# The opening of a decoder-trunk kernel: weight tiles in halves, squares summed by TensorE, two streamed columns, a new fixed order

## The chip, the cores and the metric

The kernel runs on one core of a Trainium2 chip. The time is the device time of one execution in microseconds (us). A core has four compute engines that run their own instruction lists side by side and wait for each other by semaphores: TensorE (PE: matrix products; its weight loads are listed as PEld), VectorE (DVE), ScalarE (ACT) and GpSimd (POOL). SyncE (SP) and POOL here mainly issue DMA transfers. PE writes its results into PSUM banks, which DVE and ACT read; everything else lies in SBUF, on 128 partitions.

## The reference

A trunk of two layers over 512 tokens of width 1024, all in float32. Each layer has three sub-layers, each added to the residual: a SwiGLU feed-forward, a mixing of the tokens, and a second SwiGLU feed-forward. Ahead of each stands an RMS norm whose scale and shift come from a vector `c`:

```python
c_act = jax.nn.silu(c)
for l in range(DEPTH):
    mod = (c_act @ w_ada[l] + b_ada[l]).reshape(B, N_MOD, D_MODEL)
    sh1, sc1, gt1, sh2, sc2, gt2, sh3, sc3, gt3 = [mod[:, i, None, :] for i in range(N_MOD)]
    hn = rms_norm(h, g_ffn1[l]) * (1.0 + sc1) + sh1
    h = h + 0.5 * (1.0 + gt1) * swiglu(hn, w_ffn1_in[l], w_ffn1_out[l])
    hn = rms_norm(h, g_mix[l]) * (1.0 + sc2) + sh2
    ...   # attention over a window, RWKV-7, a short convolution, side by side; w_mix_out
    hn = rms_norm(h, g_ffn2[l]) * (1.0 + sc3) + sh3
    h = h + 0.5 * (1.0 + gt3) * swiglu(hn, w_ffn2_in[l], w_ffn2_out[l])
```

The change touches only the way to the first `hn` of the first layer and the first six of the 44 output tiles of `hn @ w_ffn1_in[0]`.

## The kernel before

All activations lie transposed: `h` and `hn` are eight blocks (k = 0 to 7) of 128 columns of the model by 512 tokens. A product is made to float32's precision out of three products in a shorter format: the weight and the activation are each split into a high part (a cast on ACT) and the rest (a subtraction on DVE), and PE adds wH·xH, wH·xL and wL·xH. In the steady part `split` (lines 139 and 141) makes the parts of a weight tile of 128x1024 and `mm3` (lines 127 to 129) the three products. One output tile is thus 8 blocks times 3, or 24, matmuls of 128x128 by 512.

The opening, `begin` (line 1317 on), comes ahead of all this and is written out by hand. Its steps are tokens of a table, `PLAN`; `step` turns a token into instructions, and `pin` chains each to the one ahead of it on its engine, so that the table is the order. What the tokens do:

- `R0` spreads the 512 values 1/rms to all partitions (PE, line 1415). Ahead of it, in plain code, ACT and DVE square the blocks of `h`, DVE adds the eight squares up (line 1375), PE sums over partitions (line 1380), ACT takes the root (1382) and DVE the reciprocal of 128x4 values (1383).
- Scale and shift of the columns of block k come by one of two ways. For a *streamed* column: `ada`k multiplies c by a megabyte of `w_ada` on PE (1437), `part`k copies the sums (ACT, 1440), `col`k adds them over partitions (PE, 1444), and `gm`k finishes the scale and the shift (`finish`, DVE, lines 1389 and 1390). For a *dotted* one: `d`k and `e`k are two dot products on DVE (1394), of 128x1024 each, with `crep`, silu(c) spread to all partitions; `e`k ends with `finish` too.
- `z`k multiplies block k of `h` by 1/rms (DVE, 1420), `x`k applies scale and shift (ACT, 1422), `H`k and `L`k split the result (ACT 1424, DVE 1426).
- `wH`n and `wL`n split weight tile n (ACT 1430, DVE 1432). `P`nk and a letter is one matmul of output tile n (line 1409): a is wH·xH, b is wH·xL, c is wL·xH. There are 6 x 8 x 3 = 144 of them; the last wL·xH of the last tile ends the opening on PE, and the next tile's matmuls, of lines 127 to 129, follow.
- `W` and a number are so many products of ones, which nobody reads (line 1350). `s`k is silu over a half of `crep`. `more` names the loads that are issued behind a token.

The loads of the opening stand on SP's queue alone: `h` in four of 512 KB, eight of 1 MB of `w_ada` (`wada`) and six weight tiles of 512 KB (`wfirst`, five buffers). Behind the opening, ACT and DVE work through the splits of the next weight tiles (`wraw`), silu and products of the finished tiles (lines 520 to 524), and dot products with `w_ada` for the later norms (line 197), in an order which the program's scheduler sets from the code's order and its priorities.

Of the kernel before, what the change touches and what calls it, by code (L numbers as in the profile page):

```python
# [33 lines left out]
ada0 R0 part0 s0 col0 z0 wH0 ada1 gm0 z5 x0 z4 part1 z1 H0 W2 col1 z7 s1 P00a wH1 gm1 z3 x1 L0 W4 P10a ada2 z6 wH2 z2 H1 P00b wL2 P10b P20a part2 P20b  # L34
P01a wH3 col2 L1 P20c P11a gm2 P30a P30b wL3 x2 P01b P11b P21a P21c H2 P21b d3 P31a P30c P31b P31c P02a P12a L2 P22a P22c P32a e3 P02b P12b P22b wH4
P32c P32b wL0 W1 P40a x3 P40b P41a P41b P42a H3 P42b d4 P00c P01c P02c P03a P03c L3 P13a wH5 P23a P23c P33a e4 P03b P13b P50a P50b P51a P51b P52a wL5
x4 P52b P23b P33c P33b H4 P43a d5 P43b P50c P51c P52c P53a P53b L4 P53c P04a P04c e5 P14a P04b P14b P24a P24c P24b P34a P34c wL4 x5 P34b P44a P44b
P54a H5 P54c d6 P54b P40c P41c P42c P43c P44c L5 P05a P05c P15a e6 P05b P15b P25a P25c P25b P35a P35c wL1 P35b x6 P45a P45c P45b P55a H6 P55c d7 P10c
P11c P12c P13c P14c P15c L6 P55b P06a P06c e7 P06b P16a P16c P16b P26a P26c P26b x7 P36a P36c P36b P46a H7 P46c P46b P56a P56c L7 P56b P07a P07c P07b
P17a P17c P17b P27a P27c P27b P37a P37c P37b P47a P47c P47b P57a P57c P57b  # L40
""".split()
GROUPS = ((0, 12), (12, 22))
# [26 lines left out]
def trunk_kernel(ctx, tc, ins, out, layers=L, phases=("ffn1", "mix", "ffn2")):  # L69
# [1247 lines left out]
    def begin(pool):  # L1317
# [13 lines left out]
        wa, wf = [], []  # L1331

        def fetch():
            w = pool.tile([P, 2 * D], F32, name="wada", tag="wada", bufs=4)
            nc.sync.dma_start(w, ins["wa0"][len(wa)])
            wa.append(w)

        def fetch_w():
            j, g = divmod(len(wf), 2)
            w = pool.tile([P, KD, P], F32, name="wfirst", tag="wfirst", bufs=5)  # L1340
            nc.sync.dma_start(w, ins["w1i"][0, j, g])
            wf.append(w)
# [16 lines left out]
        for k in range(KD):  # L1359
            pin("PE", mm(turned[k // 4][:, k % 4], cT[:, k : k + 1].to_broadcast([P, P]), cst("ident"), start=True, stop=True))  # L1360
        warm(22)
        ss, sqs = new_ss(), {}
        sqs[0] = ss
        for i in range(KD):
            if i in (3, 4):
                x = pool.tile([P, T], F32, name="sqs", tag=f"sq{i}")
            else:
                x = E("sq") if i else ss
            sqs[i] = x
            if i == 3:  # L1370
                pin("DVE", tt(x, h[i], h[i], ALU.mult))
            else:
                pin("ACT", act(x, h[i], AF.Square))
        for a, b in ((0, 1), (0, 2), (0, 3), (4, 5), (4, 6), (4, 7), (0, 4)):
            pin("DVE", tt(sqs[a], sqs[a], sqs[b], ALU.add))
        for f in (fetch, fetch_w, fetch, fetch_w, fetch_w, fetch, fetch_w, fetch):
            f()
        pt = psum([P, NB], "ps_ss")
        for b in range(NB):
            pin("PE", mm(pt[:, b : b + 1], ss[:, b * P : (b + 1) * P], ones[:, :1], start=True, stop=True))  # L1380
        r = pool.tile([P, NB], F32, name="rstd_t", tag="rstd_t")
        pin("ACT", act(r, pt, AF.Sqrt, bias=vals["eps"], scale=1.0 / D))
        pin("DVE", nc.vector.reciprocal(r, r))
        rstd = psum([P, T], "ps_rstd", "r1")
        pin("DVE", stt(col["gb"], bsc, 1.0, g1, ALU.add, ALU.mult))
# [10 lines left out]
        more = {"ada0": (fetch, fetch_w), "ada1": (fetch,), "wL0": (fetch_w, fetch), "e3": (fetch,)}  # L1396

        def step(token):
            kind = "P" if token[0] == "P" else token.rstrip("0123456789")
# [3 lines left out]
            if kind == "P":  # L1403
                n, k, p = int(k[0]), int(k[1]), "abc".index(k[2])
                if n not in pts:
                    pts[n] = psum([P, T], "ps_mm", ("r0", "r1", "mm")[n % 3])
                w, x = ws[n][p == 2][:, k], weave(hn[k][p == 1])
                first, last = (token == ends[n][e] for e in range(2))
                latest["large"] = pin("PE", mm(paired(pts[n]), w, x, start=first, stop=last, skip_group_check=True))  # L1409
                return  # L1410
            k = int(k)
            c = slice(k, k + 1)
            if kind == "R":
                for b in range(NB):
                    pin("PE", mm(rstd[:, b * P : (b + 1) * P], r[:, b : b + 1].to_broadcast([P, P]), cst("ident"), start=True, stop=True))
            elif kind == "s":
                pin("ACT", act(crep[:, k * 512 : k * 512 + 512], turned[k].rearrange("p k n -> p (k n)"), AF.Silu))
# [7 lines left out]
            elif kind == "L":  # L1425
                pin("DVE", nc.vector.tensor_sub(hn[k][1], zs[k], hn[k][0].bitcast(F32)))
            elif kind == "wH":
                home, bufs = (wp, 4) if k < 4 else (pool, 2)
                ws[k] = tuple(home.tile([P, KD, P], F32R, name=x, tag=x, bufs=bufs) for x in ("wH", "wL"))
                pin("ACT", nc.scalar.copy(ws[k][0], wf[k]))  # L1430
            elif kind == "wL":
                pin("DVE", nc.vector.tensor_sub(ws[k][1], wf[k], ws[k][0].bitcast(F32)))
            elif kind == "ada":
                sums[k] = psum([P, 2 * P], "ps_ada")
                for i in range(KD):
                    j = slice(i % 4 * 32, i % 4 * 32 + 32)
                    pin("PE", mm(sums[k][j], cz[:, i], wa[k][:, i * 2 * P : (i + 1) * 2 * P], start=i < 4, stop=i >= 4))
            elif kind == "part":
                part[k] = pool.tile([P, 2 * P], F32, name="part", tag="part", bufs=2)
                pin("ACT", nc.scalar.copy(part[k], sums[k]))  # L1440
            elif kind == "col":
                sums[k] = psum([P, 2], "ps_col")
                for i in range(2):
                    pin("PE", mm(sums[k][:, i : i + 1], part[k][:, i * P : (i + 1) * P], ones[:, :1], start=True, stop=True))
            elif kind == "gm":
                finish(c, sums[k][:, :1], sums[k][:, 1:])
            elif kind == "d":
                dot(k, "sc", 0)
            elif kind == "e":
                dot(k, "sh", D)  # L1450
                finish(c, col["sc"][:, c], col["sh"][:, c])
            for f in more.get(token, ()):
                f()
# [42 lines left out]
def lay_out(i):  # L1496
# [12 lines left out]
    a["wa0"] = c(np.concatenate([streams[:3], wT[0, 1::-1, 3:].transpose(1, 2, 0, 3).reshape(5, P, 2 * D)]))  # L1509
# [67 lines left out]
```

## Time and profile before

| | |
|---|---|
| three timed runs | 1805.3, 1805.43 and 1809.03 us, median 1805.43 us |
| the profiled execution | 1807.22 us, of which the span of the profile is 1805.5 us |
| clock granted to PE, mean | 0.997 |
| PE / DVE / ACT / POOL busy | 98% / 75% / 47% / 8% of the span |
| first matmul of the opening's six tiles | starts at 19.37 us |
| last of them | starts at 59.84 us; the next section's first starts at 60.06 us |

The rows in the prediction are of a profiled execution. In a timeline a row gives the start and the duration in us, the engine, the line of the kernel, the operation, output<-input, the size, and the number of instructions that are drawn together; square brackets give the idle time before it and what ended it. PE's rows overlap: a matmul of 512 columns is shown with 0.38 us, while the next one starts 0.215 us after it. In the rows by windows the numbers are the length, the busy time of PE, its weight loads, DVE, ACT and POOL (with counts), the granted clock, the share of the DMA engines that is busy, and GB/s.

### The profile page before, as it was taken

To read this page: it belongs to the slowest core of one execution; us is meant where nothing else is said; L and a number is where in the kernel's file an instruction comes from. 1 tells how busy PE (TensorE), PEld (TensorE's weight loads), DVE (VectorE), ACT (ScalarE), POOL (GpSimd) and SP (SyncE) were. 2 spreads that over 40 slices of the span, in tenths; PEclk is the share of its full clock that TensorE was granted. 3 is DMA by queue.
4 is the path that set the end of the run, shared out by engine and by line. 5 is a ranking of instruction groups with operands and counts; after the bars stand their busy time and mean duration, and the time that the engine had idled before them with its cause. 6 is when DMAs were issued, how large, how long until landed. Compare 5 with 4: busy or idle time off the path is not lost.

```text
span 1805.5 us, 33687 instructions
## 1 busy us (share of the span) xinstructions
PE 1774.8 (98%) x13848; PEld 1616.9 (90%) x13848; DVE 1350.3 (75%) x2187; ACT 840.9 (47%) x1295; POOL 142.5 (8%) x227
## 2 busy tenths in 40 slices
PE   8999999999999999999999999999999999999999
PEld 6889899987778999899899989999876798999998
DVE  6688587877767977677888776887686788864862
ACT  5353255374443554255355524544654345533541
POOL 0101010101000001100100020110000000010000
PEclk9999999999999999999999999999999999999999
DMA  8667876623123576967737687773421427684742
GB/s 342 218 176 232 243 201 197 228 65 103 54 88 120 150 200 193 291 181 206 246 108 200 180 290 204 195 231 105 122 73 32 141 79 198 186 245 132 198 141 71
DMA packets 91405, 309.93 MB, mean 172 GB/s; under 512 B 10417, under 2 KB 11185, under 8 KB 90225
## 3 DMA queue, kind: packets, MB, share of 16 engines
q1 hardware_dynamic: 61920, 201.58, 32.9%
q0 software_dynamic: 29328, 106.18, 23.5%
q8 instruction: 109, 1.79, 0.4%
q14 instruction: 48, 0.39, 0.1%
HBM read 303.79 MB, written 3.93 MB: 170 GB/s over the span
## 4 chain that ended last, share of the span: by engine, by line
PE 81%; DVE 9%; DMA 4%; ACT 4%; issue 3%; POOL 0%; SPq 0%; ACTq 0%; DVEq 0%; POOLq 0%
PE ps_mm L127 13%; PE ps_mm L128 13%; PE ps_mm L129 13%; PE ps_d L431 7%; PE ps_d L433 7%; PE ps_d L432 7%; PE ps_f L433 3%; PE ps_f L431 3%; PE ps_f L432 3%; PE ps_g L433 2%; PE ps_g L431 2%; PE ps_g L432 2%; DVE wL L141 2%; PE ps_mm L1409 1%; ACT wH L139 1%
## 5 line engine op out<-in xcount | busy, mean ns | idle before, releaser
L139 ACT CAST wH<-wraw 128x1024 fp32r<-128x1024 f32 (+2 forms) x290 | 263.9, 916 | 465.8 <-PE ps_mm L128 212.4
L141 DVE TENSOR_TENSOR wL<-wraw,wH 128x1024 fp32r<-128x1024 f32 (+2 forms) x290 | 305.5, 1058 | 123.3 <-ACT wH L139 122.0
L127 PE MATMUL ps_mm<-actH,wH 128*128 128x512 f32 (+1 forms) x784 | 281.0, 358 | 0.0
L129 PE MATMUL ps_mm<-actH,wL 128*128 128x512 f32 (+1 forms) x784 | 280.6, 358 | 0.3 <-DVE wL L141 0.3
L128 PE MATMUL ps_mm<-actL,wH 128*128 128x512 f32 (+1 forms) x784 | 280.5, 358 | 0.0
L127 PE MATMUL ps_mm<-hnH,wH 128*128 128x512 f32 (+1 forms) x712 | 246.8, 353 | 1.7 <-ACT hnH L289 1.3
L128 PE MATMUL ps_mm<-hnL,wH 128*128 128x512 f32 (+1 forms) x712 | 246.2, 348 | 0.1
L129 PE MATMUL ps_mm<-hnH,wL 128*128 128x512 f32 (+1 forms) x712 | 244.8, 346 | 0.6 <-DVE wL L141 0.6
L431 PE MATMUL ps_d<-comH,wH 128*128 128x256 f32 x816 | 225.2, 276 | 0.8 <-ACT s L457 0.7
L432 PE MATMUL ps_d<-comL,wH 128*128 128x256 f32 x816 | 224.4, 275 | 0.0
L433 PE MATMUL ps_d<-comH,wL 128*128 128x256 f32 x816 | 224.4, 275 | 0.0
L141 DVE TENSOR_TENSOR wL<-sum,wH 128x1024 fp32r<-128x1024 f32 x102 | 124.9, 1225 | 81.0 <-ACT wH L139 80.8
L197 DVE SCALAR_TENSOR_TENSOR wada<-wada,crep 128x1024 f32<-128x1024 f32 x128 | 153.2, 1219 | 29.2 <-DMA wada<-in_wadaT 28.9
L129 PEld LDWEIGHTS ps_mm<-actH,wL 128*128 128x128 f32 x784 | 148.7, 190 | 17.5 <-DVE wL L141 0.7
L127 PEld LDWEIGHTS ps_mm<-actH,wH 128*128 128x128 f32 x784 | 148.7, 190 | 16.8 <-ACT wH L139 0.2
L128 PEld LDWEIGHTS ps_mm<-actL,wH 128*128 128x128 f32 x784 | 148.7, 190 | 16.6
L431 PEld LDWEIGHTS ps_d<-comH,wH 128*128 128x128 f32 x816 | 156.6, 192 | 2.3 <-ACT s L457 2.3
L433 PEld LDWEIGHTS ps_d<-comH,wL 128*128 128x128 f32 x816 | 156.7, 192 | 0.0
L432 PEld LDWEIGHTS ps_d<-comL,wH 128*128 128x128 f32 x816 | 156.6, 192 | 0.0
L139 ACT CAST wH<-sum 128x1024 fp32r<-128x1024 f32 x102 | 106.8, 1047 | 104.6 <-PE ps_f L432 42.4
L127 PEld LDWEIGHTS ps_mm<-hnH,wH 128*128 128x128 f32 x712 | 133.1, 190 | 22.0 <-issue 7.9
L129 PEld LDWEIGHTS ps_mm<-hnH,wL 128*128 128x128 f32 x712 | 135.4, 190 | 14.0 <-DVE wL L141 1.0
(389 smaller groups left out, 3861.0 us busy)
## 6 DMA issues: line engine op xcount, KB each, us to landing
wada<-in_wadaT POOLq DMA_DIRECT2D x128, 512.0 KB, 4.8
wraw<-in_wmi SPq DMA_DIRECT2D x40, 512.0 KB, 3.6
wraw<-in_w2p SPq DMA_DIRECT2D x36, 512.0 KB, 3.8
wraw<-in_w1p SPq DMA_DIRECT2D x32, 512.0 KB, 4.3
wraw<-in_w1o SPq DMA_DIRECT2D x32, 384.0 KB, 4.4
wraw<-in_w2o SPq DMA_DIRECT2D x32, 384.0 KB, 4.6
wraw<-in_w1o SPq DMA_DIRECT2D x32, 320.0 KB, 3.7
wraw<-in_w2o SPq DMA_DIRECT2D x32, 320.0 KB, 3.4
```

Source lines behind the costliest of these rows:

```text
L127: mm(acc, wH, xH, start=start, stop=False)
L128: mm(acc, wH, xL, start=False, stop=False)
L129: latest["large"] = mm(acc, wL, xH, start=False, stop=stop)
L139: nc.scalar.copy(hi, src)
L141: return nc.vector.tensor_sub(lo, src, hi.bitcast(F32))
L197: stt(w, w, 1.0, crep, ALU.mult, ALU.mult, accum_out=out_)
L431: mm(acc, wH, xH, start=start and i + k == 0, stop=False, skip_group_check=True)
L432: mm(acc, wH, xL, start=False, stop=False, skip_group_check=True)
L433: mm(acc, wL, xH, start=False, stop=k == 3, skip_group_check=True)
L1409: latest["large"] = pin("PE", mm(paired(pts[n]), w, x, start=first, stop=last, skip_group_check=True))
```

## The change

Eight things change, all in `begin` and in `lay_out`, the host's layout of the inputs; line numbers of the later functions move by two.

1. Weight tiles are loaded and split in halves of four blocks (128x512; token `wH3a` is the first half of tile 3): 12 loads of 256 KB instead of 6 of 512 KB, in six buffers. All loads of the opening are pinned on SP in a new order.
2. PE sums the squares: for each block four products with ones of 128x32, into four groups of 32 rows of one bank (`ps_ss`). The seven additions on DVE go. DVE squares three blocks instead of one. 1/rms is now a tile of 128x128, so the root and the reciprocal run over 128 columns instead of 4.
3. Two columns are streamed instead of three; block 2 is now dotted, which makes 12 dot products instead of 10.
4. ACT finishes scale and shift (two instructions of 128x1) instead of DVE.
5. silu is applied to c before it is spread, so `crep` is copied out plainly; the load of ACT's table for silu, formerly in the opening, comes at the first silu behind it.
6. 22 warm products ahead of the sums become 1, 2 and 5; later ones become `W2` and `W3`.
7. The six tiles' PSUM banks are (r0, r0, mm, r1, r1, mm) instead of r0, r1, mm in turn; tile 4 takes over the bank of `ps_rstd`.
8. `PLAN` is new.

```diff
-ada0 R0 part0 s0 col0 z0 wH0 ada1 gm0 z5 x0 z4 part1 z1 H0 W2 col1 z7 s1 P00a wH1 gm1 z3 x1 L0 W4 P10a ada2 z6 wH2 z2 H1 P00b wL2 P10b P20a part2 P20b
...
+R0 ada0 z2 wH1a z0 wH3a z6 part0 z7 W2 col0 wL1a gm0 x0 z1 W3 ada1 wL3a H0 z3 wH5a P10a P10c P30a z5 part1 P30c wH0a P50a wL5a col1 wH2a P00a L0 P50c
...
+HALF = {"a": slice(0, KD // 2), "b": slice(KD // 2, KD)}
+BANK = ("r0", "r0", "mm", "r1", "r1", "mm")
...
-            pin("PE", mm(turned[k // 4][:, k % 4], cT[:, k : k + 1].to_broadcast([P, P]), cst("ident"), start=True, stop=True))
-        warm(22)
...
-        for a, b in ((0, 1), (0, 2), (0, 3), (4, 5), (4, 6), (4, 7), (0, 4)):
-            pin("DVE", tt(sqs[a], sqs[a], sqs[b], ALU.add))
-        for f in (fetch, fetch_w, fetch, fetch_w, fetch_w, fetch, fetch_w, fetch):
-            f()
-        pt = psum([P, NB], "ps_ss")
-        for b in range(NB):
-            pin("PE", mm(pt[:, b : b + 1], ss[:, b * P : (b + 1) * P], ones[:, :1], start=True, stop=True))
...
+            pin("PE", mm(turned[k // 4][:, k % 4], cact[:, k : k + 1].to_broadcast([P, P]), cst("ident"), start=True, stop=True))
+        pss = psum([P, P], "ps_ss")
+        sqs = {}
         for i in range(KD):
...
+            sqs[i] = pool.tile([P, T], F32, name="sqs", tag="z", bufs=KD)
+            if i in (3, 5, 7):
+                pin("DVE", tt(sqs[i], h[i], h[i], ALU.mult))
...
+                pin("ACT", act(sqs[i], h[i], AF.Square))
+            for b in range(NB):
+                pin("PE", mm(pss[32 * b : 32 * b + 32], ones[:, :32], sqs[i][:, b * P : (b + 1) * P], start=i == 0, stop=i == KD - 1))
+            if i in (2, 4):
+                k = i // 2 - 1
+                pin("ACT", nc.scalar.copy(crep[:, k * 512 : k * 512 + 512], turned[k].rearrange("p k n -> p (k n)")))
+            if i in (3, 5):
+                warm((i - 1) // 2)
+        for token in "a0 w1a w3a a1 w5a w0a w2a a2 w4a a3".split():
+            fetch(token)
+        warm(5)
+        r = pool.tile([P, P], F32, name="rstd_t", tag="rstd_t")
...
-            pin("DVE", stt(col["gm0"][:, c], sc, g1[:, c], col["gb"][:, c], ALU.mult, ALU.add))
-            pin("DVE", tt(col["sh0"][:, c], sh, bsh[:, c], ALU.add))
+            pin("ACT", act(col["gm0"][:, c], sc, AF.Identity, bias=col["gb"][:, c], scale=g1[:, c]))
+            pin("ACT", act(col["sh0"][:, c], sh, AF.Identity, bias=bsh[:, c]))
...
-        more = {"ada0": (fetch, fetch_w), "ada1": (fetch,), "wL0": (fetch_w, fetch), "e3": (fetch,)}
+        more = {"ada0": "a4 w5b", "ada1": "a5 w4b w1b w2b", "e2": "a6 w3b w0b", "e3": "a7"}
...
-                    pin("PE", mm(rstd[:, b * P : (b + 1) * P], r[:, b : b + 1].to_broadcast([P, P]), cst("ident"), start=True, stop=True))
...
+                    pin("PE", mm(rstd[:, b * P : (b + 1) * P], cst("ident")[:, 32 * b : 32 * b + 1].to_broadcast([P, P]), r, start=True, stop=True))
...
-    a["wa0"] = c(np.concatenate([streams[:3], wT[0, 1::-1, 3:].transpose(1, 2, 0, 3).reshape(5, P, 2 * D)]))
+    a["wa0"] = c(np.concatenate([streams[:2], wT[0, 1::-1, 2:].transpose(1, 2, 0, 3).reshape(6, P, 2 * D)]))
```

The next rows are PE's list from its first instruction to the first matmul of the six tiles, before the change. `ps_crep` is the spreading of c, `ps_ss` the sum of squares, `ps_ada` and `ps_col` the two steps of a streamed column, `ps_rstd` the spreading of 1/rms.

```order
L1350 MATMUL ps_warm<-ones_r 128x512 x3
L1360 MATMUL ps_crep<-con,cT 128x128 x8
L1350 MATMUL ps_warm<-ones_r 128x512 x22
L1380 MATMUL ps_ss<-ones_r,ss 128x1 x4
L1437 MATMUL ps_ada<-wada,cz 32x256 x8
L1415 MATMUL ps_rstd<-con,rstd_t 128x128 x4
L1444 MATMUL ps_col<-ones_r,part 128x1 x2
L1437 MATMUL ps_ada<-wada,cz 32x256 x8
L1350 MATMUL ps_warm<-ones_r 128x512 x2
L1444 MATMUL ps_col<-ones_r,part 128x1 x2
L1409 MATMUL ps_mm<-hnH,wH 128x512
```

The same stretch of PE's list after the change:

```order
L1361 MATMUL ps_crep<-con,cact 128x128 x8
L1371 MATMUL ps_ss<-sqs,ones_r 32x128 x16
L1351 MATMUL ps_warm<-ones_r 128x512
L1371 MATMUL ps_ss<-sqs,ones_r 32x128 x8
L1351 MATMUL ps_warm<-ones_r 128x512 x2
L1371 MATMUL ps_ss<-sqs,ones_r 32x128 x8
L1351 MATMUL ps_warm<-ones_r 128x512 x5
L1425 MATMUL ps_rstd<-rstd_t,con 128x128 x4
L1439 MATMUL ps_ada<-wada,cz 32x256 x8
L1351 MATMUL ps_warm<-ones_r 128x512 x2
L1446 MATMUL ps_col<-ones_r,part 128x1 x2
L1351 MATMUL ps_warm<-ones_r 128x512 x3
```

The sums of squares now stand right behind the spreading of c, between a few warm products; the spreading of 1/rms stands ahead of the first streamed column instead of behind it, and the second column's `ps_ada` (the next row, not shown) comes behind the first column's `ps_col`.

On DVE, the rows right behind the opening before the change are these. `wL` is the rest of a weight tile's split, `silu` and `actL` belong to the finished output tiles, and `mod` is a result of the dot products with `w_ada` for a later norm:

```order
L141 TENSOR_TENSOR wL<-wraw,wH 128x1024
L522 SCALAR_TENSOR_TENSOR silu<-silu,ps_mm 128x512 x3
L524 TENSOR_TENSOR actL<-silu,actH 128x512 x3
L141 TENSOR_TENSOR wL<-wraw,wH 128x1024 x2
L197 SCALAR_TENSOR_TENSOR wada,mod_2_571<-wada,crep 128x1024 x3
L221 TENSOR_TENSOR mod_2_571<-mod_2_571,par 128x2
L141 TENSOR_TENSOR wL<-wraw,wH 128x1024
```

And after it:

```order
L143 TENSOR_TENSOR wL<-wraw,wH 128x1024
L524 SCALAR_TENSOR_TENSOR silu<-silu,ps_mm 128x512 x3
L526 TENSOR_TENSOR actL<-silu,actH 128x512
L143 TENSOR_TENSOR wL<-wraw,wH 128x1024
L526 TENSOR_TENSOR actL<-silu,actH 128x512
L199 SCALAR_TENSOR_TENSOR wada,mod_2_582<-wada,crep 128x1024
L526 TENSOR_TENSOR actL<-silu,actH 128x512
L199 SCALAR_TENSOR_TENSOR wada,mod_2_582<-wada,crep 128x1024 x2
L223 TENSOR_TENSOR mod_2_582<-mod_2_582,par 128x2
L143 TENSOR_TENSOR wL<-wraw,wH 128x1024
```

The split of the third weight tile behind the opening, which stood right behind the second's, now stands behind the three dot products.

More of the change, by code (lines that the diff above doesn't have):

```diff
@@ L1409, in step @@
                 latest["large"] = pin("PE", mm(paired(pts[n]), w, x, start=first, stop=last, skip_group_check=True))
+                return
+            if kind in ("wH", "wL"):
+                n, part_ = int(k[0]), HALF[k[1]]
+                if n not in ws:
+                    home, bufs = (wp, 4) if n < 4 else (pool, 2)
+                    ws[n] = tuple(home.tile([P, KD, P], F32R, name=x, tag=x, bufs=bufs) for x in ("wH", "wL"))
+                wH, wL, w = (x[:, part_] for x in (*ws[n], wf[n]))
+                if kind == "wH":
+                    pin("ACT", nc.scalar.copy(wH, w))
+                else:
+                    pin("DVE", nc.vector.tensor_sub(wL, w, wH.bitcast(F32)))
                 return
@@ L1445, in step @@
             elif kind == "gm":
-                finish(c, sums[k][:, :1], sums[k][:, 1:])
+                finish(c, *((sums[k][:, :1], sums[k][:, 1:]) if k in sums else (col["sc"][:, c], col["sh"][:, c])))
             elif kind == "d":
@@ L1450, in step @@
                 dot(k, "sh", D)
-                finish(c, col["sc"][:, c], col["sh"][:, c])
-            for f in more.get(token, ()):
-                f()
+            for load in more.get(token, "").split():
+                fetch(load)
         ends = {n: [[t for t in PLAN if t[:2] == f"P{n}"][e] for e in (0, -1)] for n in range(6)}
```

59 lines of the change are left out of this document (20 added, 39 removed).

## The prediction

> **What bounds the kernel now.** PE is busy for 98% of the span, so I first asked where it stands still or does what need not be done. The chain of waits, cut to the opening, gives the one long piece that is not PE's:
>
> ```profile
> 24.29 11.93 DMA wfirst<-in_w1i
> 36.24 1.05 ACT wH L1430
> 37.33 21.61 PE ps_mm L1409 x91
> ```
>
> The sixth weight tile is awaited for 12 us; behind its cast PE runs to the end of the opening without a break. Next I read PE's timeline up to there:
>
> ```profile
> 2.38 1.65 PE L1350 MATMUL ps_warm<-ones_r 128*128 128x512 f32 x3 [2.38 <-ACT ones_r L165]
> 3.83 3.43 PE L1360 MATMUL ps_crep<-con,cT 128*128 128x128 f32 x16
> 7.01 5.29 PE L1350 MATMUL ps_warm<-ones_r 128*128 128x512 f32 x22
> 12.49 1.05 PE L1380 MATMUL ps_ss<-ones_r,ss 128*128 128x1 f32 x8 [0.18 <-DVE ss L1375]
> 13.47 1.07 PE L1437 MATMUL ps_ada<-wada,cz 128*32 128x256 f32 x16
> 14.47 1.16 PE L1415 MATMUL ps_rstd<-con,rstd_t 128*128 128x128 f32 x8
> ...
> 18.85 0.61 PE L1444 MATMUL ps_col<-ones_r,part 128*128 128x1 f32 x4 [1.14 <-ACT part L1440]
> 19.37 0.48 PE L1409 MATMUL ps_mm<-hnH,wH 128*128 128x512 f32 x1
> 19.69 1.09 PE L1350 MATMUL ps_warm<-ones_r 128*128 128x512 f32 x4
> ...
> 22.75 1.07 PE L1437 MATMUL ps_ada<-wada,cz 128*32 128x256 f32 x16 [1.46 <-DMA wada<-in_wa]
> ...
> 24.93 0.50 PE L1444 MATMUL ps_col<-ones_r,part 128*128 128x1 f32 x4
> ...
> 31.09 0.48 PE L1409 MATMUL ps_mm<-hnH,wH 128*128 128x512 f32 x1 [0.36 <-ACT wH L1430]
> ...
> 37.33 0.52 PE L1409 MATMUL ps_mm<-hnH,wH 128*128 128x512 f32 x1 [2.31 <-ACT wH L1430]
> ...
> 46.25 1.24 PE L1409 MATMUL ps_mm<-hnH,wL 128*128 128x512 f32 x5
> ...
> 60.06 0.38 PE L127 MATMUL ps_mm<-hnH,wH 128*128 128x512 f32 x1
> ```
>
> The first of the 144 real matmuls starts at 19.37, the next section's first at 60.06: 40.7 us. Where they run densely, five take 1.24 us and one alone shows 0.38, so the pace is (1.24 - 0.38)/4 = 0.215 us, and 144 of them need 31.0 us. The other 9.7 are: the third streamed column (about 1.4 with its `ps_col`), five warm products (1.3), waits of 1.46, 0.36 and 2.31, some small ones, and this, from the windows:
>
> ```profile
> 37.50:41.00 3.50, 3.50 (x9) 2.82 (x10) 3.50 (x5) 1.12 (x2) 0.00 (x0) 0.52 0.83 328
> 41.00:50.00 9.00, 9.00 (x43) 7.83 (x42) 9.00 (x20) 2.87 (x4) 0.00 (x0) 1.00 0.02 5
> ```
>
> Behind the wait of 2.31 us the granted clock was 0.52 for 3.5 us, so nine matmuls ran where sixteen would have: about 1.7 us. So the wait for the last weight tile cost some 4 us. The opening is thus bound by loads and the order around them, not by PE's work, and up to 9.7 us, plus an earlier start, can be won.
>
> **Part by part: the start.** The prices come from these rows of ACT and DVE, the last of a view that groups equal shapes:
>
> ```profile
> 5.16 0.29 ACT L1357 ACTIVATE sh<-cact,v_eps 128x1 f32<-128x1 f32 x1
> ...
> 8.50 1.90 ACT L1373 ACTIVATE sq<-h 128x512 f32<-128x512 f32 x3
> 13.58 0.26 ACT L1382 ACTIVATE rstd_t<-ps_ss,v_eps 128x4 f32<-128x4 f32 x1 [3.17 <-PE ps_ss L1380]
> ...
> 18.44 0.36 ACT L1440 COPY part<-ps_ada 128x256 f32<-128x256 f32 x1
> ...
> 37.19 0.81 ACT L1422 ACTIVATE z<-z,sh,gm 128x512 f32<-128x512 f32 x1
> 38.03 0.62 ACT L1424 CAST hnH<-z 128x512 fp32r<-128x512 f32 x1
> ```
>
> ```profile
> 11.74 0.69 DVE L1375 TENSOR_TENSOR ss<-ss,sqs 128x512 f32<-128x512 f32 x1
> 13.87 0.18 DVE L1383 RECIPROCAL rstd_t<-rstd_t 128x4 f32<-128x4 f32 x1 [1.44 <-ACT rstd_t L1382]
> ```
>
> ```profile
> L772 DVE RECIPROCAL rq<-ps_rq 128x32 f32<-128x32 f32 x2 | 0.7, 356 | 0.2
> ```
>
> Before, ACT's squares end at 10.4 and DVE's additions at 12.43. After, PE starts on the sums when `ps_crep` ends, at about 7.0 (the third of ACT's and DVE's squares are there by then). Eight sets of four products are new. Nearest is `ps_ada`, which also writes groups of 32 rows: eight products of 256 columns in 1.07 us. By count a set costs 0.53, by columns 0.27; if the groups did not overlap, `ps_rstd` (four full products in 1.16) is the upper end. I take 0.53: the groups' rows are those of `ps_ada`, the columns fewer. With three warm products that is 4.9 us, to 11.9; the squares (by 10) are not last. The root of 128 columns costs between 0.26 (4) and 0.36 (256): 12.3. The reciprocal costs 0.18 for 4 columns and 0.356 for 32, 6.3 ns a column, so 0.96 for 128: 13.25; if it does not go on in a line, up to 2 us. `R0` (1.16) ends at 14.4, against 15.63 before. Then one streamed column in a row: `ada0` 1.0, `part0` 0.36, `col0` 0.5, two finishing instructions of 0.29 that partly overlap (0.55), `x0` 0.75, `H0` 0.6, with the gaps 4.0: first real matmul at **18.4**, 1.0 earlier. By the other ends of the sets it would be 16.9 or, at 1.16 a set, 23.5.
>
> **The 144 matmuls.** In the new order they need 31.0 us, with one `ps_col` between them (0.36) and small waits, for which I take 0.9, as much as the small ones of before: 18.4 + 31.0 + 1.3 = **50.7**, instead of 60.06. That holds if nothing else ends later, so I went through DVE and the loads:
>
> ```profile
> 16.47 2.47 DVE L1420 TENSOR_TENSOR z<-h,ps_rstd 128x512 f32<-128x512 f32 x4
> ...
> 25.67 1.22 DVE L1432 TENSOR_TENSOR wL<-wfirst,wH 128x1024 fp32r<-128x1024 f32 x1
> 26.80 1.22 DVE L1394 SCALAR_TENSOR_TENSOR wada<-wada,crep 128x1024 f32<-128x1024 f32 x1
> ...
> 51.62 0.69 DVE L1426 TENSOR_TENSOR hnL<-z,hnH 128x512 fp32r<-128x512 f32 x1 [1.53 <-ACT hnH L1424]
> ```
>
> ```profile
> GB/s 16 276 397 437 408 429 410 423 415 419 411 428 418 421 403 403 69 0 7 0 0 182 28 0 256 398 405 415 385 267 341 280 216 208 356 139 120 120 249 126
> ```
>
> DVE's list from `R0` on is 8 `z` and 8 `L` of 0.62, 12 dot products of 1.15, 12 half splits of about 0.6: 30.9 us. From 14.4 it ends at 45.3 without a wait. Its last product, `L7`, is first needed three matmuls after `P07a` begins, 16 matmuls (3.4 us) before the end, at 47.2. So DVE has 1.9 us for waits; it is the next bound behind PE. The loads: 400 to 430 GB/s in each slice of 2.5 us until 40, so 512 KB take 1.25 us and a half 0.63. The bytes stay the same, so the last `w_ada` block lands by 39.4, as before (two tiles of the next section come behind it and the queue runs dry shortly after 40). From there: `e7` 1.2, finishing 0.55, `x7`, `H7` 1.35, up to 1.3 of queueing, and the 18 matmuls of block 7 behind `H7`, 3.9: 47.7. This too lies under 50.7. The tight place in the middle is block 2, now dotted: DVE's list brings `d2` at 22.4, its load is there at 22.1 (the third `wada` block was awaited until 22.75 as the last of 4.5 MB, and is now the last of 4.25); `d2`, `L1`, `e2`, finishing, `x2` and `H2` end at 27.2, and 36 matmuls stand ahead of `P02a`, which PE could reach at 26.5. So 0.7 of the 0.9 that I took for waits is here. `P40a`, which now waits for `z4` because of the banks, comes at 25.2 and `z4` ends about 25.9: the same wait. The finishing costs ACT 16 x 0.25 = 4 us more and frees DVE of 16 x 0.14; ACT has gaps of some 3 us ahead of each dotted column's `x`, so it hides there, except for the 0.3 to 0.5 counted in the chains. SP's six more issues hide behind the full queue. The opening brings **-9.4 us**.
>
> **Behind the opening.** DVE's order there is new:
>
> ```profile
> 62.93 2.35 DVE L141 TENSOR_TENSOR wL<-wraw,wH 128x1024 fp32r<-128x1024 f32 x2
> 66.20 1.22 DVE L197 SCALAR_TENSOR_TENSOR wada<-wada,crep 128x1024 f32<-128x1024 f32 x1 [0.93 <-DMA wada<-in_wadaT]
> ...
> 70.33 0.16 DVE L221 TENSOR_TENSOR mod<-mod,par 128x2 f32<-128x2 f32 x1
> ```
>
> ```profile
> 70.85 0.38 PE L129 MATMUL ps_mm<-hnH,wL 128*128 128x512 f32 x1
> ...
> 119.88 0.38 PE L431 MATMUL ps_d<-comH,wH 128*128 128x256 f32 x1 [0.72 <-ACT s L457]
> ```
>
> The third raw weight tile's `wL` used to be the second of the two at 62.93, done at 65.3; now it comes behind the three dot products, at 70.4 to 71.6 in these times, and PE needs it at 70.85: a wait of about 0.8. Each later split of that stretch comes one slot, 1.2 us, later, and at 119.88 PE already waits for the vector engines. ACT loads its table for silu there, too, which took this in the opening:
>
> ```profile
> 15.00 1.28 ACT L1417 ACT_TABLE_LOAD   x1
> ```
>
> It makes the first silus 1.28 us later, and with them the next `wL`; that one has some 1.8 to spare. Between 0.8 (the first wait alone) and 4.4 (1.2 more at each of three later waits) I take 1.8, near the lower end, since PE's later waits for DVE are 0.7 each and partly give way. Net **-7.6 us**. The profiled execution (1807.22, span 1805.5) lies 1.8 above the median; a difference carries over, so 1805.43 - 7.6 = **1797.8** for a median (1799.6 by the profiled one).
>
> **A rule against it.** The Trainium skill ("DMA: Bandwidth & Descriptors", "Anatomy of one DMA") gives a transfer about 2.0 us plus its bytes at 436 GB/s, 2.6 us for a half; the row of GB/s speaks against it for a full queue, since 512 KB loads would then move at 164 GB/s and move at over 400. By the rule alone the opening would end at 71.3, as reckoned in D, and the time be near 1818. What 256 KB loads do no row shows.
>
> **The rivals.** A measurement here can tell about 0.2%, 3.6 us, from no change.
>
> *A, as summed*: 1797.8; own range 1795 to 1800.5. Chance 0.62.
>
> *B, a cold clock at the start.* Three warm products fill 2.38 to 3.83, 0.48 each instead of 0.215, and `ps_crep` takes 0.43 each, where `ps_rstd` of the same shape took 0.29: PE starts slow, and before, 22 warm products follow. They become eight between small ones. If the clock stays at half until about 3.5 us into the real matmuls, `R0` and `ada0` cost 1.1 and 1.0 more and eight matmuls 0.215 each: +3.8, or 1801.6. For it: the wait of 2.31 sufficed for a slow clock. Against: those of 1.14 and 1.46 did not. By the Trainium skill ("TensorE: Matmul & The Clock Gate", "What's actually happening") half rate is the default, and a busy window of about 3.4 us lifts it; the rows from 2.38 on agree as far as they go. Chance 0.13.
>
> *C, DVE behind the opening*: the splits stay late at every wait, 4.4 instead of 1.8: 1800.4; with two more DVE waits of 1 us in the opening beyond its 1.9, 1801.5. Chance 0.11.
>
> *D, slower: the loads in halves.* If a half costs more than 0.63 in the queue, by d, the last block lands 12 d later, and the opening ends at 47.7 + 12 d. It decides from d = 0.25; at d = 0.88 (1.51 us a half) the end is 58.3, which the 1.8 behind makes no change; slower by over 0.2% from d = 1.18 (1.81 a half). At 2 us a half: 64.1, +5.8: 1811. Against it: the rates of that row. Chance 0.06.
>
> *E, no change: the next section does not start earlier.* Its dot products already wait 0.93 us for `in_wadaT`, loaded by POOL in its own time; if those loads and the raw tiles come when they came, PE stands by what the opening won: 1804 to 1806. Against: the wait is short, and in the opening the raw tiles were issued some 25 us ahead. Chance 0.08.
>
> **How the numbers follow.** The prediction is A's. From below, cheap sets of squares (-1.5), no waits (-0.9) and nothing given back (-1.8) make 1793.6; from above, B and C reach 1801.6, and a unit beyond holds their spread: 1793.5 to 1802.5, leaving out D, E and edges. Faster by over 0.2% (under 1801.8): A, most of C, half of B, together 0.79. Same: the rest of B and C and most of E, 0.13. Slower: D and some of E, 0.08.
>
> **What would show it.** Right: the first real matmul at 18 to 19, no wait over 1 us and no clock under 1 between it and the next section's first matmul, which starts near 50.7; `L7` done 1 to 3 us ahead of `P07b`; DVE the releaser of one new PE wait at the third raw tile. Wrong: sets of `ps_ss` near 1 us, loads of 256 KB under 350 GB/s, a granted clock near 0.5 behind the first matmul, or a next section's first matmul that starts early and waits as long.

## The result, and the profile after

The changed kernel took 1803.68 us at the median of 22 runs, the kernel before 1807.24 at the median of 22 beside it: a ratio of 0.998 (95% interval 0.9973 to 0.9987), about 3.6 us or 0.2% less. Forecast were 7.6 us less, 1797.8 in a range of 1793.5 to 1802.5. The sign was right, and the size was half of what was forecast; the median lies above the range. One of the 22 runs of the changed kernel, 2015.24 us at a granted clock of 0.85, is left out of the ratio.

The profiled execution took 1800.83 us, with a span of 1798.9. Its PE timeline, from the first sums of squares to the third raw weight tile behind the opening:

```profile
7.21 1.08 PE L1371 MATMUL ps_ss<-sqs,ones_r 128*32 128x128 f32 x32
...
12.13 1.16 PE L1425 MATMUL ps_rstd<-rstd_t,con 128*128 128x128 f32 x8
13.22 1.07 PE L1439 MATMUL ps_ada<-wada,cz 128*32 128x256 f32 x16
...
17.48 0.48 PE L1408 MATMUL ps_mm<-hnH,wH 128*128 128x512 f32 x1 [0.28 <-ACT hnH L1432]
...
50.14 0.46 PE L129 MATMUL ps_mm<-hnH,wH 128*128 128x512 f32 x1
...
63.29 0.48 PE L131 MATMUL ps_mm<-hnH,wL 128*128 128x512 f32 x1 [2.12 <-DVE wL L143]
...
111.63 0.38 PE L435 MATMUL ps_g<-hnH,wL 128*128 128x256 f32 x1 [1.48 <-DVE wL L143]
```

The first real matmul starts 1.9 us earlier than before (17.48 against 19.37), and the next section's first, of line 129, 9.9 us earlier (50.14 against 60.06). Between them lies no wait of a microsecond. The window over this stretch shows it, with a granted clock of 1.00 where before it fell to 0.52:

```profile
17.40:50.10 32.70, 32.49 (x148) 27.26 (x148) 28.09 (x48) 22.90 (x44) 0.70 (x1) 1.00 0.78 314
```

Then the gain shrinks. The row at 63.29 is the same product as that at 70.85 before: 7.6 us earlier only, since PE now waits 2.12 us for it. What it waits for is in the timeline of ACT and of DVE:

```profile
48.17 1.28 ACT L522 ACT_TABLE_LOAD   x1
49.47 1.58 ACT L522 ACTIVATE silu<-ps_mm 128x512 f32<-128x512 f32 x3
```

```profile
57.11 1.23 DVE L199 SCALAR_TENSOR_TENSOR wada<-wada,crep 128x1024 f32<-128x1024 f32 x1 [2.75 <-DMA wada<-in_wadaT]
...
60.80 1.22 DVE L199 SCALAR_TENSOR_TENSOR wada<-wada,crep 128x1024 f32<-128x1024 f32 x1 [0.70 <-DMA wada<-in_wadaT]
...
62.02 1.22 DVE L143 TENSOR_TENSOR wL<-wraw,wH 128x1024 fp32r<-128x1024 f32 x1
```

DVE stands idle for 2.75 us ahead of the first dot product, whose load has not landed, with the third tile's split queued behind the three dot products. The weight itself had been cast before. The loads themselves were not asked for late. POOL's timeline has the issue of the first three in the kernel before, and in the changed kernel:

```profile
60.92 1.59 POOL L208 DMA_DIRECT2D wada<-in_wadaT  x3 [7.59 <-ACT silu L520]
```

```profile
51.01 1.58 POOL L210 DMA_DIRECT2D wada<-in_wadaT  x3 [4.66 <-ACT silu L522]
```

They come 9.9 us earlier, as the opening's end does, and land 0.8 us (the first) to 1.5 us (the third) later behind their issue. At the end of the program the lead over the first profile of before is 6.4 us, but 6.4 is not what the times show.

### The profile page after: what moved, and what is told of

Same layout as the page of the kernel before. It is cut to its first block, busy times and chain, and to the rows that moved or that the text cites. A ratio compares the mean times of both kernels' runs of the same rounds, so it can differ in the third digit from the quotient of the medians.

```text
span 1798.9 us, 33741 instructions
## 1 busy us (share of the span) xinstructions
PE 1769.2 (98%) x13868; PEld 1611.8 (90%) x13868; DVE 1349.2 (75%) x2176; ACT 845.8 (47%) x1314; POOL 142.4 (8%) x227
## 4 chain that ended last, share of the span: by engine, by line
PE 76%; DVE 10%; DMA 6%; ACT 4%; issue 3%; POOL 0%; SPq 0%; ACTq 0%; POOLq 0%; DVEq 0%
PE ps_mm L129 11%; PE ps_mm L130 11%; PE ps_mm L131 11%; PE ps_d L433 7%; PE ps_d L434 7%; PE ps_d L435 7%; PE ps_f L434 3%; PE ps_f L435 3%; PE ps_f L433 3%; DMA wada<-in_wadaT 2%; DVE wL L143 2%; DVE wada L199 2%; PE ps_g L435 2%; PE ps_g L434 2%; PE ps_g L433 2%
```

## The experiments

Two theories stood at the start. T1: the wait of 2.1 us makes the clock fall in most executions, which costs 3 to 5 us more. T2: what varies lies elsewhere. Later runs looked for the rest of the loss. A *lead* below is how much earlier the same PE row starts than in the first profile of before.

**The changed kernel again** (no edit).

> The changed kernel again, for a second profile and more times. Theory T1: in most executions the clock granted to PE falls behind the 2.1 us wait at the third raw weight tile (about 61 to 63 us), which costs 3 to 5 us on top of the wait; a profile of such an execution shows a granted clock near 0.5 between 60 and 70, and its time is near 1804, not 1800. Rival T2: the times vary by 7 us because of waits elsewhere (the RWKV stages at 490 and 1380 us, or the start); then the clock is 1.0 from 60 to 70 whatever the time.

Measured: 1802.7 us (12 runs), ratio to before 0.998 (0.9968 to 0.9993). The profiled execution took 1804.12. Its opening and its wait at the third tile are as in the first profile (1.94 us), with a clock of 1.00 there. So T1 does not explain this slower execution. It waited elsewhere, as the waits between 750 and 990 us show:

```profile
PE ps_mm L131 <- DVE wL L143: 1.1, 1, 1.1
PE ps_ss L273 <- ACT sq L254: 1.1, 1, 1.1
```

**ACT's table for silu loaded in the opening.**

```diff
+        pin("ACT", act(col["sc"][:, :1], col["gb"][:, :1], AF.Silu))
         nc.sync.dma_start(con[:, P:], ins["con"][:, P:])
```

> The changed kernel with one silu of a 128x1 column at the end of the opening's list on ACT, so that the table for silu is loaded in ACT's gap of 2.5 us there and not behind the first raw cast; by that the third raw tile's split also stands ahead of the dot products again. T1: the PE wait of 2.1 us goes, the clock stays up, and the time is 1797 to 1799.5 at the median with a spread under 5 us, about 4 to 6 below the changed kernel. T2: only the wait goes, 1.5 to 2 us below the changed kernel, with its spread of 7 us.

Measured: 1800.43 us (10 runs), ratio to before 0.997 (0.9959 to 0.998), where the changed kernel had 0.998 on the same chip; 2.3 us less, nearer to T2, and with a spread of 6.8 us. ACT's timeline shows the load in the gap, DVE's the third split (the second of the two at 53.27) ahead of the dot products:

```profile
44.89 1.28 ACT L1459 ACT_TABLE_LOAD   x1
...
48.32 1.08 ACT L522 ACTIVATE silu<-ps_mm 128x512 f32<-128x512 f32 x2
```

```profile
53.27 2.35 DVE L143 TENSOR_TENSOR wL<-wraw,wH 128x1024 fp32r<-128x1024 f32 x2
57.05 1.23 DVE L199 SCALAR_TENSOR_TENSOR wada<-wada,crep 128x1024 f32<-128x1024 f32 x1 [1.42 <-DMA wada<-in_wadaT]
```

PE's wait at the third tile is gone. The loads of the dot products are issued no earlier (51.27 against 51.01), and the dot products start no earlier (57.05 against 57.11). Moving the table's load, listed in the change as a side effect of applying silu earlier, thus had two effects: 1.28 us on ACT, and another order by the scheduler. This run undoes both at once; the next one parts them.

**The order alone.** The table is loaded late, as in the changed kernel.

```diff
         latest["w"] = split(wH[:, :n], wL[:, :n], w[:, :n], behind)
+        subs.append(latest["w"])
+        if len(subs) == 3:
+            tc.add_manual_dep(dots[0].ins, latest["w"].ins.name, ORDER, reason="the third split first")
```

> The changed kernel with one order alone: the third raw tile's split on DVE ahead of the dot products; ACT's table is still loaded behind the first raw cast. If the order of the two makes the wait: the wait of 2.1 us at the third raw tile goes, and the time is that of the kernel with the table loaded early within 1 us. If the table's 1.28 us makes it: a wait of about 1 us stays. T1: spread under 5 us; T2: as the changed kernel.

Measured: 1797.83 us (6 runs), ratio to before 0.9962 (0.9949 to 0.9974). DVE's timeline has the split done at 56.7, ahead of the first dot product, and PE does not wait:

```profile
55.48 1.22 DVE L143 TENSOR_TENSOR wL<-wraw,wH 128x1024 fp32r<-128x1024 f32 x1
56.86 1.23 DVE L200 SCALAR_TENSOR_TENSOR wada<-wada,crep 128x1024 f32<-128x1024 f32 x1 [0.16 <-DMA wada<-in_wadaT]
```

So the order made the wait; the table's 1.28 us alone, still there, makes none at that tile. The time was expected within 1 us of the run before; it is 2.6 us lower, with intervals that overlap, and nothing here explains that.

**Whole tiles.** Each weight tile is loaded whole where its first half was.

```diff
-                pin("SP", nc.sync.dma_start(wf[n][:, HALF[token[2]]], ins["w1i"][0, n // 2, n % 2][:, HALF[token[2]]]))
+                    pin("SP", nc.sync.dma_start(wf[n], ins["w1i"][0, n // 2, n % 2]))
```

> The changed kernel with the weight tiles loaded whole (512 KB at the place of the first half), all else as it is, splits in halves too. If halves matter by what they let pass (my reading): the third w_ada block has 1.28 MB more ahead of it, lands 3 us later, the dotted column 2 comes 3 us later and the opening ends 2.5 to 3.5 us later, with a PE wait ahead of the first matmuls of block 2. If a load of 256 KB costs more in the queue than half a load of 512 KB, the end comes back by that: 12 halves at 0.1 us more each would make it 1 us less. If the opening doesn't hang on these loads: no difference.

Measured: 1805.76 us (12 runs), ratio to before 1.0002 (0.9993 to 1.0012): the whole gain in time is gone, though the opening still ends 6.0 us earlier than before. PE's timeline:

```profile
20.44 0.48 PE L1408 MATMUL ps_mm<-hnH,wH 128*128 128x512 f32 x1 [1.03 <-ACT wH L1417]
21.72 0.48 PE L1408 MATMUL ps_mm<-hnH,wH 128*128 128x512 f32 x1 [0.40 <-ACT wH L1417]
22.97 0.79 PE L1408 MATMUL ps_mm<-hnH,wH 128*128 128x512 f32 x1 [0.55 <-ACT wH L1417]
...
54.03 0.46 PE L129 MATMUL ps_mm<-hnH,wH 128*128 128x512 f32 x1
```

The opening ends 3.9 us later than with halves, somewhat more than expected. The waits are for the first weight tiles, not for block 2, though its first dot product starts at 24.80 instead of 21.73. Behind them the clock fell, as the windows of this execution show (granted clock 0.60 and 0.55):

```profile
22.00:24.00 2.00, 1.45 (x5) 0.86 (x5) 1.04 (x2) 1.66 (x4) 0.00 (x0) 0.60 1.05 426
24.00:26.00 2.00, 2.00 (x7) 1.59 (x6) 1.45 (x4) 0.79 (x2) 0.00 (x0) 0.55 1.00 414
```

That is 4 x 0.425 or 1.7 us of the 3.9; the waits are about 2. Halves let the order start PE on many tiles early without such waits. They are not free: from 5 to 40 us the loads ran at 416 GB/s here, as in all four profiles of before, and at 407 to 409 in the seven of the changed kernel. For the same bytes that is about 0.7 us, an estimate of 0.06 us a half, which this kernel had to spare.

**Further profiles.** Two of the kernel before, one of the changed one, one of the order alone.

> The kernel before, for a second profile. So far the changed kernel and its variants lose 1 to 2.6 us against the one profile of before between 880 and 912 us, where the order of all engines is the same. If this loss belongs to the change (theory S: an earlier opening shifts loads against PE there), this profile shows PE without a wait of over 0.3 us from 880 to 912, as the first one. If it is chance in the landing of weight tiles (theory R), this profile has waits of its own there or at other just-in-time places (200, 350, 760, 893, 906), 1 to 3 us in sum.

> The same once more. Theory S: again no wait from 880 to 912 and the slow clock at 37 to 41 us. Theory R: waits there that differ from profile to profile.

> The changed kernel, a third profile: the opening ends at 50.1 to 50.2 as twice before, the third raw tile's wait is 2 us again; theory R: the sum of small waits behind it differs by 1 to 4 us from the two others.

> The third split ahead of the dot products, a second profile. Five of six runs lay at 1796.8 to 1798.4, the profiled one at 1801.4. If it is one of the five: the lag behind the opening stays near -9 us up to 345, and the waits between 345 and the end are 2 to 3 us fewer than in the first profile.

Measured: before 1810.5 and 1806.96 us, and 1810.2 for one more execution beside them; the changed kernel 1801.27, the order alone 1798.92. Theory R holds: the second profile of before has waits of 0.8 and 0.4 us between 880 and 912, the third none there, but each loses some 2 us between 1045 and 1240 us, where the first profile lost nothing; the third wins most of that back by 1400 us, where the first lost it. So small losses come and go in both kernels, and one pair of profiles can't rank them. The order alone kept a lead of 8.4 us at 345 us and lost none of it behind, 2 us less than in its first profile, much as expected. The wait of 2.3 us and the slow clock behind it are in every profile of before.

**The same chip for four.** The changed kernel once more; the wait filled with work; the order alone once more; scale and shift finished on DVE.

> The changed kernel on the chip of the three that follow, so that they stand against it. The traces so far make it 6 us faster than before, the times 3 us; 1802 to 1804 if before is at 1805.5 to 1807. If the clock falls behind the third raw tile's wait in most executions (T1), a fourth profile has a chance of over half to show it; four without would speak against it.

Measured: 1803.45 us (12 runs), ratio 0.9979 (0.9967 to 0.9991). This profile, 1800.37 us, does show the clock fall of T1, in the windows behind a wait of 2.33 us:

```profile
64.00:66.00 2.00, 2.00 (x8) 1.63 (x8) 2.00 (x5) 0.00 (x0) 0.53 (x1) 0.72 0.97 299
66.00:68.00 2.00, 2.00 (x7) 1.55 (x5) 1.32 (x4) 0.62 (x1) 0.00 (x0) 0.50 0.68 227
```

and still it is the fastest of the seven. PE's wait for `wL` at 111.63 is missing in it, as in the other profile with the fall (1803.76 us, below), while the five without it wait 0.7 to 1.6 us there. I read this as time that PE would have waited for DVE anyway. So T1's fall is real, in two of seven profiles, but most of it is hidden.

```diff
         acc = paired(acc)
+        for _ in range(fill):
+            mm(acc, wH, xH, start=True, stop=True)
         mm(acc, wH, xH, start=start, stop=False)
```

> The changed kernel with nine more matmuls, whose sum the next one overwrites, ahead of the tile whose third product waits 2.1 us: PE is busy in that time, and the end of the wait stays where it is. T1 (the clock falls there in most timed executions and costs 3 us): the time comes down by 2 to 3 us against the changed kernel. Rival: only the wait of 2.1 itself costs, and filled it costs the same: within 1 us of the changed kernel.

Measured: 1799.16 us (7 runs), ratio 0.9966 (0.9951 to 0.9981); mean 1799.9 against 1802.5 for the changed kernel, 2.6 less with a standard error of about 1.2 (from deviations of 2.2 and 2.9). PE was busy from 58 to 70 us at a clock of 1.00. That is what T1 expects, but the profiled execution (1802.2) shows no gain anywhere behind, and a few swaps on ACT and DVE between 90 and 115 us came with the edit. The granted clocks of the timed executions, 0.9980 in the mean against 0.9972, are worth 1.5 us with an error of about 1.1, which leans the same way. I count it as unclear.

> The third raw tile's split ahead of the dot products, once more, on the same chip as the changed kernel. The traces give 2.0 to 2.3 us at that place. If that is all: 2 to 2.5 us under the changed kernel. If the wait also costs clock later: 4 to 5 us under it, as the first times suggest.

Measured: 1799.15 us (10 runs), ratio 0.9958 (0.9945 to 0.9971), 4.3 under the changed kernel on the same chip, which by the medians is the upper of the two readings. By the means it is 3.6 with a standard error of about 1.1, which does not part them well; with the first chip's 4.2 it is 3.9 with an error of about 0.8. In three profiles with this order the lead at 118 us is 8.7 to 9.5, against 6.3 to 8.0 in the seven of the changed kernel.

```diff
-            pin("ACT", act(col["gm0"][:, c], sc, AF.Identity, bias=col["gb"][:, c], scale=g1[:, c]))
-            pin("ACT", act(col["sh0"][:, c], sh, AF.Identity, bias=bsh[:, c]))
+            pin("DVE", stt(col["gm0"][:, c], sc, g1[:, c], col["gb"][:, c], ALU.mult, ALU.add))
+            pin("DVE", tt(col["sh0"][:, c], sh, bsh[:, c], ALU.add))
```

> The changed kernel with scale and shift finished on DVE again (16 instructions, two for each column, at their old places behind the dot products). My reading: DVE is the next bound of the opening; its list grows by 8 x 0.28 = 2.2 us, of which its slack before L7 takes 1 to 2, so the opening ends 0 to 1.2 us later. Rival: each column comes earlier, because two ACT instructions of 0.3 leave the chain of each column; then the opening ends up to 0.5 us earlier.

Measured: 1802.3 us (12 runs), ratio 0.9979 (0.9968 to 0.999). The opening ends at 51.27, 1.1 us later, inside what I expected; the time cannot be told from the changed kernel's. The reason is not the one expected, for PE's timeline shows that 0.8 of it comes at the first matmul already:

```profile
18.28 0.48 PE L1408 MATMUL ps_mm<-hnH,wH 128*128 128x512 f32 x1 [1.02 <-ACT hnH L1432]
...
51.27 0.46 PE L129 MATMUL ps_mm<-hnH,wH 128*128 128x512 f32 x1
```

The two instructions stand behind half a weight split in DVE's list there, and the scale comes at 16.39 instead of 15.43. `L7` is done 1.8 us later (47.12 against 45.34), still 0.7 us ahead of the matmul that needs it, and PE does not wait for it.

**Where the rest goes.** Three more profiles of the changed kernel and one of before.

> The changed kernel, a fifth profile. If the further loss sits at the just-in-time tiles: of the profiles from here on, those with times over 1803 lose 2 us more than those under 1801 between 118 and 912. If it is the clock: those over 1803 have more stretches of 3.4 us at a granted clock of 0.5.

> The changed kernel, a sixth profile. The same two readings: a time over 1803 goes with more loss at the tiles between 118 and 912, or with more stretches at half clock.

> The changed kernel, a seventh profile. The same two readings; if all seven lie near 1801, the loss of the timed executions stays without a trace.

> The kernel before, a fourth profile: the wait of 2.3 us and the slow clock at 37 to 41 again; loss from 118 to the end 0 to 3.5 us against its first profile, as in the two others.

Measured: 1804.27, 1801.28, 1803.76, and 1810.57 for before, with 1806.97 for one more execution of before beside them. The seven profiles of the changed kernel, by time (the waits are PE's, from the view of waits cut to 750 to 990 us; the leads as defined above):

| time, us | wait at the third tile | lead at 118 us | waits 750 to 990 us | lead at the end |
|---|---|---|---|---|
| 1800.37 | 2.33, clock falls | 6.3 | none | 6.8 |
| 1800.83 | 2.12 | 6.8 | 1.2 | 6.4 |
| 1801.27 | 1.72 | 7.4 | none | 6.0 |
| 1801.28 | 0.97 | 8.0 | 0.2 | 5.9 |
| 1803.76 | 2.02, clock falls | 6.8 | 2.7 | 3.5 |
| 1804.12 | 1.94 | 7.8 | 2.2 | 3.1 |
| 1804.27 | 0.42 | 8.0 | 1.5 | 2.9 |

The first reading fits. The three above 1803 wait 1.5 to 2.7 us between 750 and 990, the four others 0 to 1.2; neither the third tile nor the clock there sorts them. The second reading is not excluded: the granted clock of the whole execution is 0.997 to 0.999 in the four and 0.995 to 0.998 in the three. The waits view of the execution of 1803.76 us names what is late:

```profile
PE ps_ss L273 <- ACT sq L254: 1.3, 1, 1.3
PE ps_mm L129 <- ACT wH L141: 1.1, 1, 1.1
PE ps_mm L131 <- DVE wL L143: 0.3, 1, 0.3
```

These are weight tiles just in time, and the norm sum at the end of the first layer, whose square waits on ACT and DVE behind such a tile's split.

## Why the prediction was wrong

**The opening: right.** It ends at 50.14, predicted 50.7; -9.9 us, predicted -9.4. Without the long wait there is no slow clock. Within it two terms were off in opposite directions. A set of four sums of squares costs 0.27 us (1.08 for four sets), the lower bound by columns, where I took 0.53 by count. At that price the sums keep pace with the squares, which I had called not last: the last ones end at 10.02 (DVE's first row below) and the last two sets behind them at 10.65, not 11.9. So `R0` starts at 12.13 and the first matmul at 17.48 instead of 18.4. The matmuls then take 32.7 us instead of 32.3. The reciprocal of 128 columns, on which I had only rows of 4 and 32, came out as the straight line said. PE's last sums, and DVE's rows:

```profile
10.01 0.64 PE L1371 MATMUL ps_ss<-sqs,ones_r 128*32 128x128 f32 x16
```

```profile
9.33 0.69 DVE L1367 TENSOR_TENSOR sqs<-h 128x512 f32<-128x512 f32 x1 [0.61 <-DMA h<-in_xT]
...
11.12 0.95 DVE L1383 RECIPROCAL rstd_t<-rstd_t 128x128 f32<-128x128 f32 x1 [1.03 <-ACT rstd_t L1382]
...
21.73 1.23 DVE L1393 SCALAR_TENSOR_TENSOR wada<-wada,crep 128x1024 f32<-128x1024 f32 x1 [0.41 <-DMA wada<-in_wa]
...
44.65 0.69 DVE L1434 TENSOR_TENSOR hnL<-z,hnH 128x512 fp32r<-128x512 f32 x1 [0.65 <-ACT hnH L1432]
```

`d2` came at 21.73 (22.4 predicted) and waited 0.41 for its load. `L7` ended at 45.3, the time that I had summed, but that is partly luck: DVE's list began 1.1 us earlier than I took it to, and lost as much in two waits (0.41 and 0.65 above). It was done 1.35 us ahead of the first matmul that needs it, where I had 1.9. Whether DVE is the next bound is not shown: finishing on DVE moved the end by 1.1, but mostly at the first matmul.

**Rival D, halves dear in the queue: wrong in size.** The GB/s by slices of 2.5 us are 358 to 433 from 5 to 40 us, 408 in the mean against 416 before, and the queue runs dry some 0.7 us later:

```profile
GB/s 19 269 413 430 383 430 358 395 433 429 419 389 424 406 398 398 193 3 98 111 228 256 379 390 241 264 305 344 308 216 208 75 395 174 141 285 0 182 229 218
```

That is about 0.06 us a half, far from the 0.25 at which D begins to count. The 2 us that the Trainium skill gives each transfer ("DMA: Bandwidth & Descriptors", "Anatomy of one DMA") do not show here; the section states them for transfers that GpSimd issues, and these loads are SP's, six more than before, in a full queue. **Rival B, a cold clock at the start**, did not come in the profiles of the changed kernel: the clock is 1.00 from 17 to 50 us in them.

**The step that failed: "I take 1.8" behind the opening.** This term stood for all that is given back there; the traces give back 2.6 by 118 us and 5.0 by the end, at the mean of seven profiles. The place of the first wait was right and its mechanism too: the third raw tile's `wL` behind three dot products. The size was not. I priced PE's wait from the times of one profile of before, 70.4 to 71.6 against 70.85. But those times hang on when the dot products' loads land. In that profile the first and third dot product start 5.3 and 7.2 us behind the issue of their loads; here it is 6.1 and 8.7, so they start only 9.1 (57.11 against 66.20) to 8.4 us (60.80 against 69.18) earlier, not 9.9, with the split in DVE's queue behind them. The other three profiles of before have 5.1 to 6.0 and 7.2 to 8.9, so I had taken a price from an execution whose loads landed early, and moved it as if it were fixed. Why the landing varies is not shown. PE's wait became 1.7 to 2.3 us in five of seven profiles instead of 0.8; the shortest, 0.42, comes with the earliest landing (5.0 and 7.0). By 118 us the lead is 7.3 at the mean, so 2.6 of 9.9 were given back there, more than the 1.8 I had for all. That later splits come late too, as I had feared, does not show as a cost of the order: around 111 us the lead shrinks by 0.3 to 0.5 us also with the third split first, against 0.6 in the mean of the five profiles of the changed kernel without the clock's fall. The table's load, which I looked at only for the next `wL`, cost nothing at that tile by itself; it cost by changing the scheduler's order.

**What was not in the sum.** From 118 us to the end the seven lose another 2.4 us at the mean (7.3 to 4.9), between a gain of 0.5 and a loss of 5, 1.7 of it between 750 and 990 us. The engines' lists are the same there in both kernels. A difference of profiles does not simply "carry over": the program has just-in-time places that add 0 to 3 us in one execution and not in the next. Rival C's price, 4.4, comes near the 5.0 of the traces, but by luck: it stood for splits that stay late at each wait, and the loss came at other tiles. The times imply 6.3 (9.9 less 3.6). Also, the median of three runs from which I subtracted, 1805.43, lay 1.8 below the later one of 22. Together, 4.5 more given back and 1.8 of the baseline, less 0.5 by which the opening was better, make 5.8 of the 5.9 us by which the forecast missed.

The granted clock of each timed execution, which is on record too, goes with its time. Of the changed kernel's 21 runs in the ratio, the eight at 0.998 or more took 1798.97 to 1802.47 us, the thirteen at 0.996 or 0.997 took 1803.32 to 1806.81. One stretch of 3.5 us at half clock, as in the rows of before, costs 1.7 us or 0.001 of the mean clock. So slow stretches make much of the spread, more than the seven profiles suggest; which waits bring them is not shown.

**What stays open.** The four profiles of before, taken on several chips, lie at 1806.96 to 1810.57, 1808.8 in the mean, where its timed runs have medians of 1805.6 to 1807.2, so the profiles alone make the change 6.5 us and the times 3.6 (2.9 and 2.6 at the medians on two other chips). The clock is part of this: on those two chips the timed runs of before lost 3.8 and 4.6 us to it in the mean, those of the changed kernel 4.8 and 5.1 (span times what is missing from the granted clock), and without that loss the kernels are 4.3 us apart on both. Whether the changed kernel meets the waits of 750 to 990 more often than before (1.1 us at the mean of seven against 0.45 of four) is not settled by so few. With the third split first, the medians are 4.9 and 4.3 us below the changed kernel on two chips (the means 4.2 and 3.6), where the trace shows 2 at that place. The granted clocks of the timed runs give 1.8 and 1.0 us more; that the wait at the third tile brings this slower clock is not shown, and the filled wait only hints at it.

The version that beats both kernels is the changed one with the third split first: 0.9962 and 0.9958 of before.

## What to carry to other kernels

When a step is moved out of a hand-ordered part, look at what the scheduler then does behind it: here one table load of 1.28 us, moved to the first silus, came with another order on DVE, and the order cost some 2 us at a tile where the load alone cost none. Price a wait in the shifted program with its own releasers, and from several profiles, not by the times of one: here loads that landed 0.8 to 1.5 us later raised it from 0.8 to 2.1. A gain of 10 us at the start of a program of 1.8 ms reaches the end only as far as no later place is already just in time, so forecast it with a spread of a few us, compare several profiles before naming the place, and look at the granted clock of each timed run.

## What the hardware showed that I had not expected

A clock fall behind a wait of 2.0 to 2.3 us is not certain: in seven profiles of the changed kernel with waits of 0.4 to 2.3 us it came twice (at 2.02 and 2.33, not at 2.12 or 1.94), and behind 2.31 to 2.33 us in all four of before. There it is not certain either: two of 27 timed executions of before on one chip have a granted clock of 1.000 over the whole span, which leaves no room for a fall. And where PE next waits for another engine, it may cost nothing: one of the two executions with the fall was the fastest of seven. Sums over partitions in four groups of 32 rows go at 0.27 us for four products of 128 columns, a quarter of what four products over all rows took (1.16 in `ps_rstd`).
